# Hybrid decoder trunk on one core: the low part of every third weight tile of the mixers built by ScalarE and an accumulating DMA

## The chip, the cores and the metric

The kernel runs on one core of a Trainium2 chip. The metric is the device time of one execution in microseconds, from runs of the same program; lower is better. All profile rows come from one profiled execution.

## The reference

Two layers of a decoder trunk on 256 tokens of width 2048, all in float32. Each layer projects the normalised input once, feeds three token mixers (latent attention, a diagonal state-space layer with a GLU, dilated windowed attention), projects their normalised outputs back, and ends with a gated feed-forward block.

```python
def rms_norm(x, g):
    xf = x.astype(jnp.float32)
    y = xf * lax.rsqrt(jnp.mean(xf * xf, axis=-1, keepdims=True) + NORM_EPS)
    return (y * g.astype(jnp.float32)).astype(x.dtype)
...
for l in range(DEPTH):
    h = rms_norm(x, g_mix[l])
    proj = h @ w_in[l]
    c_q, c_kv, k_rope, u, qd, kd, vd = jnp.split(proj, split_at, axis=-1)
    y_mla = mla_mixer(c_q, c_kv, k_rope, g_q[l], w_uq[l], g_kv[l], w_ukv[l])
    y_ssm = s5_mixer(u, a_re[l], a_im[l], b_re[l], b_im[l], c_re[l], c_im[l],
                     d_skip[l], log_dt[l], w_glu[l], b_glu[l])
    y_dil = dilated_mixer(qd, kd, vd)
    y = jnp.concatenate([rms_norm(y_mla, g_out_mla[l]),
                         rms_norm(y_ssm, g_out_ssm[l]),
                         rms_norm(y_dil, g_out_dil[l])], axis=-1)
    x = x + y @ w_o[l]
    h = rms_norm(x, g_ffn[l])
    x = x + (jax.nn.silu(h @ w_gate[l]) * (h @ w_up[l])) @ w_down[l]
return rms_norm(x, g_final)
```

The three mixers are left out here: latent attention has 8 heads and low-rank projections `w_uq` and `w_ukv`; the state-space layer has 32 groups of 16 channels, a scan over the tokens, a GELU and the GLU weights `w_glu`; the dilated attention has 8 heads and three strides.

## The kernel before, in words

**Weights in two parts.** TensorE multiplies in a reduced float32 format (`float32r`). To keep float32 accuracy each operand is split into a high part, which is the operand rounded to that format, and a low part, which is the rest. `product` (L1347) makes three matmuls for each: high x high, high activation x low weight, low activation x high weight.

**Tiles and stripes.** Every weight matrix is cut into tiles of 256 rows by up to 512 columns, 720 in all. A `Stripe` is a run of tiles that accumulates one block of output columns for both halves of the tokens. `layer` (L1140) lists the stripes of a layer: first the mixers' in the order of `ORDER` (L1137), then the feed-forward's. A layer has 96 mixer tiles and 264 feed-forward tiles; tiles 0 to 95 and 360 to 455 belong to mixers. In layer 0 the stripes of `w_uq` and `w_ukv` are tiles 24 to 35, those of `w_o` for the attention 60 to 75 and for the dilated heads 76 to 83, the two GLU stripes (`g1 g0`) 84 to 87, and `w_o` for the state-space output 88 to 95.

**The pipeline of a tile.** `dma` (L1238) loads a raw tile on SP's queue into one of three buffers `wr` (`RAW`, L205). `wsplit` (L1248) takes one of four buffers each for `wh` and `wl` (`SPL`) and calls `split` (L333): ScalarE copies the raw tile to `wh`, VectorE subtracts `wh` from the raw tile and writes `wl`.

```python
            nc.scalar.activation(hi, src, AF.Copy)
            nc.vector.tensor_tensor(lo, src, hi.bitcast(F32), OP.subtract)
```

In `run` (L1260) the split of tile i + 3 is written in the middle of tile i's matmuls, and the load of the next raw tile right behind it. So a raw buffer is free again when the split of the tile in it is done, and a `wh`/`wl` buffer when TensorE is done with the tile four before.

**Side work and its planner.** The mixers themselves (transposes, attention heads, the state-space steps of `ssm`, L717, the norms) are generators that `spawn` puts on a list. Between the matmuls of weight tiles `run_side` (L285) takes the next step of a generator when its inputs are ready by the clock of a planner, `Pace` (L87), and when VectorE and ScalarE aren't too far behind TensorE by that clock (`busy`, L277). `order` (L259) sorts by how much time is left until a stripe needs the result. When a stripe needs something that isn't there, `drain` (L316) writes all the steps that are still missing ahead of the stripe's matmul. `Pace.op` (L148) books every instruction on the planner's clock; a changed booking changes the order in which side work is written on all engines. Nothing else orders it: each engine runs its instructions as written.

**Other queues.** POOL runs the Newton steps of the reciprocal roots (`rstd`, L352, twelve small instructions each), a few memsets, and eight loads. All operations are recorded at one line, L194 (a wrapper around each engine), so groups of the profile are told apart by the names of their tiles: `wr`, `wh`, `wl` for weights, `acc` for the accumulators, `pt` and `y` for the PSUM tiles of side work (`y` is the output of the state-space steps), `s` for work tiles, `one` for constants and small statistics.

## Time and profile before

| what | value |
|---|---|
| median of 3 runs | 2236.85 us (2236.36 to 2238.12) |
| the profiled execution | 2235.52 us |
| its span in the profile | 2233.5 us |
| TensorE matmul (PE) busy | 2184.5 us (98%) |
| weight load (PEld) busy | 1777.3 us (80%) |
| VectorE (DVE) busy | 1338.6 us (60%) |
| ScalarE (ACT) busy | 1046.1 us (47%) |
| GpSimd (POOL) busy | 100.5 us (5%) |
| mean granted TensorE clock | 0.992 |
| moved by DMA | 387.33 MB, 173 GB/s on average |

The profiled execution lies 1.3 us under the median. The busy times are sums over the span: an engine that is idle while another sets the pace costs nothing. The mixers of layer 0 end near 390 us; those of layer 1 lie between about 1140 and 1490 us; the rest is feed-forward.

### The profile page before, as it was taken

What the parts mean: (1) busy time and instruction counts of PE and PEld (TensorE: products, weight loads), DVE (VectorE), ACT (ScalarE), POOL (GpSimd) and SP (SyncE); (2) the same over time, 40 slices, a digit from 0 to 9 for tenths busy, and PEclk for the clock granted to TensorE, in tenths of its full rate; (3) what the DMA queues carried; (4) which work ended last, traced back from release to release, by engine and by line L of the source; (5) the groups of instructions that cost most, each with busy time, mean ns of one, the idle gap of its engine ahead of it and who ended that gap; (6) DMA issues with size and microseconds to landing.
All of it is one profiled execution on the core that took longest, in us unless ns stands there. A gap on an engine that the chain in (4) does not pass through costs nothing.

```text
span 2233.5 us, 27208 instructions
## 1 busy us (share of the span) xinstructions
PE 2184.5 (98%) x10127; PEld 1777.3 (80%) x10127; DVE 1338.6 (60%) x1967; ACT 1046.1 (47%) x1535; POOL 100.5 (5%) x283
## 2 busy tenths in 40 slices
PE   8899998999999999999999999999999999999998
PEld 6677876888788888888877778878888888888886
DVE  6976777658555445444568776674455545454555
ACT  6556433544534443344454555554444444434443
POOL 6100100000000000000001000010000000000000
PEclk9999999999999999999999999999999999999999
DMA  6443433656656655566554343456655666556654
GB/s 214 143 128 104 169 123 124 189 187 206 201 196 189 189 190 192 193 189 192 184 169 120 118 124 122 142 179 197 189 189 190 212 192 189 188 194 192 189 188 151
DMA packets 201012, 387.33 MB, mean 173 GB/s; under 512 B 12064, under 2 KB 20512, under 8 KB 200880
## 3 DMA queue, kind: packets, MB, share of 16 engines
q1 hardware_dynamic: 199696, 381.34, 53.6%
q0 software_dynamic: 1184, 4.26, 0.6%
q8 instruction: 79, 1.29, 0.2%
q14 instruction: 53, 0.43, 0.1%
HBM read 383.46 MB, written 2.10 MB: 173 GB/s over the span
## 4 chain that ended last, share of the span: by engine, by line
PE 87%; DVE 5%; ACT 2%; DMA 2%; POOL 2%; issue 2%; SPq 0%; DVEq 0%; ACTq 0%; POOLq 0%
PE acc L194 79%; PE pt L194 6%; PE y L194 3%; DVE s L194 3%; DVE wl L194 2%; POOL s L194 1%; ACT s L194 1%; ACT wh L194 1%; DMA s<-in_bT_dram 0%; POOL tn L194 0%; DMA wr<-in_w_up_dram 0%; DVE one L194 0%; DMA one<-in_params_dram 0%; DMA wr<-in_w_uq_dram 0%; DVE tn L194 0%
## 5 line engine op out<-in xcount | busy, mean ns | idle before, releaser
L194 PE MATMUL acc<-wh,s 128*128 128x512 f32 (+2 forms) x5760 | 1818.7, 391 | 12.4 <-ACT s L194 7.5
L194 DVE TENSOR_TENSOR wl<-wr,wh 128x1024 fp32r<-128x1024 f32 (+1 forms) x720 | 867.9, 1209 | 707.0 <-ACT wh L194 705.1
L194 PEld LDWEIGHTS acc<-wh,s 128*128 128x128 f32 x5760 | 1082.5, 189 | 238.7 <-issue 12.2
L194 PE MATMUL acc<-wl,s 128*128 128x512 f32 (+2 forms) x2880 | 1117.9, 388 | 9.7 <-DVE wl L194 9.7
L194 ACT ACTIVATE wh<-wr 128x1024 fp32r<-128x1024 f32 (+1 forms) x720 | 750.0, 1046 | 741.6 <-PE acc L194 692.5
L194 PEld LDWEIGHTS acc<-wl,s 128*128 128x128 f32 x2880 | 543.5, 189 | 116.8 <-DVE wl L194 14.3
L194 ACT ACTIVATE s<-pt 128x512 fp32r<-128x512 f32 (+6 forms) x138 | 68.6, 504 | 146.5 <-PE pt L194 145.9
L194 PE MATMUL pt<-one,s 128*128 128x128 f32 (+1 forms) x668 | 102.6, 273 | 12.2 <-DVE s L194 8.3
L194 PEld LDWEIGHTS pt<-one,s 128*128 128x128 f32 (+1 forms) x668 | 82.4, 140 | 36.4 <-issue 10.0
L194 DVE TENSOR_TENSOR s<-pt,s 128x512 f32<-128x512 f32 (+1 forms) x108 | 71.4, 685 | 56.3 <-ACT s L194 51.0
L194 ACT ACTIVATE s<-s 128x512 f32<-128x512 f32 (+4 forms) x162 | 80.0, 501 | 48.4 <-DVE s L194 32.1
L194 DVE TENSOR_TENSOR s<-s,s 128x512 f32<-128x512 f32 (+3 forms) x152 | 83.4, 587 | 8.9 <-ACT s L194 8.2
L194 ACT ACTIVATE s<-pt,tn 128x128 f32<-128x128 f32 (+2 forms) x128 | 44.4, 375 | 94.1 <-DVE tn L194 86.0
L194 ACT ACTIVATE s<-acc,one 128x512 f32<-128x512 f32 (+3 forms) x112 | 63.0, 604 | 36.0 <-PE acc L194 25.0
L194 PE MATMUL y<-s,one 128*32 128x256 f32 (+1 forms) x320 | 77.4, 389 | 1.0 <-DVE s L194 1.0
L194 ACT ACTIVATE s<-pt,one 128x256 fp32r<-128x256 f32 x108 | 45.9, 471 | 65.7 <-PE pt L194 65.7
L194 DVE SCALAR_TENSOR_TENSOR s<-pt,one,s 128x256 fp32r<-128x256 f32 x108 | 47.7, 478 | 40.7 <-ACT s L194 40.5
L194 DVE SCALAR_TENSOR_TENSOR s<-acc,one,s 128x512 f32<-128x512 f32 x92 | 64.5, 743 | 11.5 <-POOL one L194 11.5
L194 POOL TENSOR_TENSOR tn<-one 128x2 f32<-128x2 f32 x39 | 15.8, 406 | 1210.2 <-DVE one L194 1208.2
L194 PEld LDWEIGHTS y<-s,one 128*32 128x32 f32 (+1 forms) x320 | 33.1, 112 | 36.9 <-issue 6.9
L194 PE MATMUL pt<-s,s 128*128 128x128 f32 (+2 forms) x288 | 53.6, 309 | 2.3 <-ACT s L194 2.2
L194 PEld LDWEIGHTS pt<-s,s 128*128 128x128 f32 (+1 forms) x288 | 43.1, 193 | 7.6 <-ACT s L194 3.0
(74 smaller groups left out, 442.3 us busy)
## 6 DMA issues: line engine op xcount, KB each, us to landing
wr<-in_w_gate_dram SPq DMA_DIRECT2D x176, 512.0 KB, 3.6
wr<-in_w_up_dram SPq DMA_DIRECT2D x176, 512.0 KB, 3.5
wr<-in_w_down_dram SPq DMA_DIRECT2D x176, 512.0 KB, 4.3
wr<-in_w_in_dram SPq DMA_DIRECT2D x80, 512.0 KB, 3.6
wr<-in_w_o_dram SPq DMA_DIRECT2D x64, 512.0 KB, 3.7
wr<-in_w_uq_dram SPq DMA_DIRECT2D x16, 384.0 KB, 3.3
wr<-in_w_in_dram SPq DMA_DIRECT2D x16, 320.0 KB, 3.1
wr<-in_w_ukv_dram SPq DMA_DIRECT2D x8, 512.0 KB, 3.9
```

The source lines that it names most:

```text
L194: return f(out, *a, **k)
```

## The change

For a chosen tile, ScalarE writes the negative of the raw tile, rounded to float32r, into the low buffer; POOL issues a DMA that reads the raw tile and adds it to the low buffer in SBUF; ScalarE then copies the raw tile to the high buffer as before. VectorE's subtraction of that tile is gone. Chosen are the mixer tiles from 24 on whose number is divisible by three: 24 in layer 0, 32 in layer 1. The planner gets a booking of its own for such a DMA.

```diff
--- before.py
+++ after.py
@@ -147,7 +147,17 @@
 
     def op(self, e, op, out, ins, extra):
         st = self.t[e]
-        if op == "dma_start":
+        if op == "dma_start" and ins and ins[0].tensor.name in self.wrote:
+            for a in ins + [out]:
+                for l, h, w, we in self.wrote.get(a.tensor.name, ()):
+                    st = max(st, w + self.LAG)
+            self.t[e] = st + 900
+            n = 8
+            for s in out.shape:
+                n *= s
+            self.t["dma"] = max(self.t["dma"], st + 1000) + n / 400.0
+            end = self.t["dma"] + 1500
+        elif op == "dma_start":
             st = max(st, self.avail.get(out.tensor.name, 0.0))
             self.t[e] = st + 600
             n = 4
@@ -203,6 +213,7 @@
 
 class Trunk:
     RAW, SPL = 3, 4
+    BY_DMA = (24, 3)
 
     def __init__(self, tc, I, out, ctx, layers=DEPTH, dbg=None):
         self.pace = Pace()
@@ -1177,6 +1188,7 @@
                         out.append(Stripe(wo[1536:2048], 4, 512 * c, 512,
                                           lambda k, b: self.act4([self.dh], [self.dl])(k, b),
                                           self.o_done(l, c, "rd", then), f"dil{l}", col=c))
+        mixer = len(out)
         s0 = 0
         for gi, n in enumerate((4, 4, 3)):
             for s in range(s0, s0 + n):
@@ -1197,8 +1209,8 @@
                 out.append(Stripe(I["w_down"][l][s0 * 512:(s0 + n) * 512], 4 * n, 512 * c, 512, act,
                                   self.o_done(l, c, None, then if gi == 2 else None), f"hid{l}", 4 * s0))
             s0 += n
-        for st in out:
-            st.l = l
+        for i, st in enumerate(out):
+            st.l, st.mixer = l, i < mixer
         return out
 
     def start(self):
@@ -1254,7 +1266,12 @@
         l = self.sb.tile([128, 2, F], F32R, name=self.nm("wl"), tag="wl", bufs=self.SPL, padded_shape=[128, 2, 512])
         self.pace.alloc("wh", self.SPL, h)
         self.pace.alloc("wl", self.SPL, l)
-        self.split(h, l, r)
+        if i in self.by_dma:
+            self.nc.scalar.activation(l, r, AF.Copy, scale=-1.0)
+            self.nc.gpsimd.dma_start(l.bitcast(F32), r, accum_op=OP.add)
+            self.nc.scalar.activation(h, r, AF.Copy)
+        else:
+            self.split(h, l, r)
         self.hl_w[i] = (h, l)
 
     def run(self):
@@ -1270,6 +1287,12 @@
             self.left[f"ssm{l}"], self.left[f"dil{l}"], self.left[f"mla{l}"] = NP, 4, 4
         self.tiles = [(st.w, k, st.c0, st.F) for st in prog for k in range(0, st.kc, 2)]
         PS = self.SPL - 1
+        self.by_dma, i = set(), 0
+        for st in prog:
+            for k in range(0, st.kc, 2):
+                if i >= self.BY_DMA[0] and st.mixer and i % self.BY_DMA[1] == 0:
+                    self.by_dma.add(i)
+                i += 1
         self.setup()
         self.z = self.s4([640], BF)
         nc.vector.memset(self.z, 0.0)
```

The change moves instructions, because the planner books the chosen tiles differently. On TensorE, at the end of layer 0's mixers before the change (`wh_3389` is tile 85, the second tile of the stripe `g1`; `y` rows are state-space output):

```order
L194 MATMUL acc_3424<-wh_3389,s_1466 128x512
L194 MATMUL acc_3424<-wl_3390,s_1466 128x512
L194 MATMUL acc_3424<-wh_3389,s_1467 128x512
L194 MATMUL y_2963<-s_3303,one_85 32x256
L194 MATMUL y_2963<-s_3304,one_85 32x256 x2
L194 MATMUL y_2963<-s_3303,one_85 32x256
L194 MATMUL y_2963<-s_3183,one_86 32x256
L194 MATMUL y_2963<-s_3434,one_85 32x256
L194 MATMUL y_2963<-s_3435,one_85 32x256 x2
L194 MATMUL y_2963<-s_3434,one_85 32x256
L194 MATMUL y_2963<-s_3351,one_86 32x256
L194 MATMUL acc_3423<-wh_3389,s_1466 128x512
```

The last two of the sixteen state-space steps stand back to back inside the stripe that needs them. In the changed kernel the last `y` rows of layer 0 stand here (`wh_3068` is tile 70, `wh_3092` tile 71, both in the last `w_o` stripe of the latent attention):

```order
L204 MATMUL acc_3085<-wh_3068,s_1433 128x512
L204 MATMUL acc_3085<-wl_3069,s_1433 128x512
L204 MATMUL acc_3085<-wh_3068,s_1434 128x512
L204 MATMUL y_2515<-s_3038,one_85 32x256
L204 MATMUL y_2515<-s_3039,one_85 32x256 x2
L204 MATMUL y_2515<-s_3038,one_85 32x256
L204 MATMUL y_2515<-s_2947,one_86 32x256
L204 MATMUL acc_3084<-wh_3092,s_1433 128x512
```

The step has moved from tile 85 to tile 71. Behind it the listing has only matmuls of weight tiles until four transposes ahead of tile 88.

On SP's queue, the raw loads of tiles 84 to 90 before the change; DVE is the wait for the subtraction that frees the buffer, DMAHW a wait for an earlier load:

```order
L194 DMA wr_3286<-in_w_glu_dram 128x2x512 [waits DMAHW5_49,DVE_49]
L194 DMA wr_3312<-in_w_glu_dram 128x2x512 [waits DMAHW6_49,DVE_49]
L194 DMA wr_3334<-in_w_glu_dram 128x2x512 [waits DMAHW7_49,DVE_49]
L194 DMA wr_3371<-in_w_glu_dram 128x2x512 [waits DMAHW0_49,DVE_49]
L194 DMA wr_3393<-in_w_o_dram 128x2x512 [waits DMAHW1_49,DVE_49]
L194 DMA wr_3413<-in_w_o_dram 128x2x512 [waits DMAHW2_49,DVE_49]
L194 DMA wr_3443<-in_w_o_dram 128x2x512 [waits DMAHW3_49,DVE_49]
```

The same loads in the changed kernel; DMASW is a wait for a DMA that POOL issued, Activation one for ScalarE:

```order
L204 DMA wr_3373<-in_w_glu_dram 128x2x512 [waits DMAHW6_49,DVE_49]
L204 DMA wr_3391<-in_w_glu_dram 128x2x512 [waits DMAHW5_49,DMASW0_49]
L204 DMA wr_3413<-in_w_glu_dram 128x2x512 [waits DMAHW7_49,DVE_49]
L204 DMA wr_3432<-in_w_glu_dram 128x2x512 [waits DMAHW0_49,DMASW1_49,Activation_49]
L204 DMA wr_3454<-in_w_o_dram 128x2x512 [waits DMAHW1_49,DVE_49]
L204 DMA wr_3472<-in_w_o_dram 128x2x512 [waits DMAHW2_49,DVE_49]
L204 DMA wr_3495<-in_w_o_dram 128x2x512 [waits DMAHW3_49,DMASW2_49,Activation_49]
```

One load in three now waits for the accumulating DMA of a chosen tile. Tiles 87 and 90, chosen themselves, take the buffer of the chosen tile before them (84, 87); tile 84 takes one that VectorE has freed, and tile 85 behind it waits for the DMA of tile 81. In the listing the first pattern holds for 44 chosen tiles, the second for 12.

## Rows read from the trace of the kernel before

**Rows 1.** The page, busy time of each engine in the span.
```profile
PE 2184.5 (98%) x10127; PEld 1777.3 (80%) x10127; DVE 1338.6 (60%) x1967; ACT 1046.1 (47%) x1535; POOL 100.5 (5%) x283
```

**Rows 2.** By stage: length, PE, PEld, DVE, ACT, POOL busy; PEclk, DMA share, GB/s.
```profile
120.00:180.00 60.00, 59.83 (x323) 48.12 (x322) 40.26 (x94) 38.03 (x93) 3.12 (x6) 1.00 0.40 120
300.00:360.00 60.00, 54.15 (x239) 39.97 (x238) 48.31 (x94) 19.14 (x32) 2.91 (x13) 0.94 0.39 137
```

**Rows 3.** Timeline of PE, 318 to 375 us: start, us, instruction [idle before <-releaser].
```profile
323.12 0.69 PE L194 MATMUL pt<-one,s 128*128 128x128 f32 x2 [2.03 <-ACT s L194]
...
355.18 2.52 PE L194 MATMUL y<-s,one 128*32 128x256 f32 x10 [0.96 <-DVE s L194]
360.38 0.79 PE L194 MATMUL acc<-wh,s 128*128 128x512 f32 x1 [2.67 <-ACT s L194]
...
370.13 0.30 PE L194 MATMUL pt<-one,s 128*128 128x128 f32 x1 [1.16 <-DVE s L194]
371.37 0.55 PE L194 MATMUL pt<-one,s 128*128 128x128 f32 x3 [0.94 <-DVE s L194]
```

**Rows 4.** By stage as rows 2, finer, around those waits.
```profile
320.00:325.00 5.00, 2.41 (x12) 1.65 (x11) 3.13 (x11) 2.25 (x8) 0.00 (x0) 0.76 0.31 105
325.00:330.00 5.00, 5.00 (x14) 3.93 (x13) 3.01 (x7) 1.31 (x2) 1.02 (x6) 0.56 0.28 105
360.00:370.00 10.00, 8.59 (x30) 6.63 (x30) 6.71 (x9) 4.54 (x6) 0.00 (x0) 0.83 0.31 107
```

**Rows 5.** Groups of the page: xcount | busy us, mean ns | idle before <-releaser.
```profile
L194 DVE TENSOR_TENSOR wl<-wr,wh 128x1024 fp32r<-128x1024 f32 (+1 forms) x720 | 867.9, 1209 | 707.0 <-ACT wh L194 705.1
L194 ACT ACTIVATE wh<-wr 128x1024 fp32r<-128x1024 f32 (+1 forms) x720 | 750.0, 1046 | 741.6 <-PE acc L194 692.5
```

**Rows 6.** Timeline of PE near 101 us.
```profile
101.44 0.45 PE L194 MATMUL pt<-one,s 128*128 128x128 f32 x1 [5.29 <-DVE s L194]
```

**Rows 7.** DMA issues: queue, xcount, KB each, median us from issue to landing.
```profile
wr<-in_w_in_dram SPq DMA_DIRECT2D x80, 512.0 KB, 3.6
...
s<-in_x_dram POOLq DMA_DIRECT2D x4, 512.0 KB, 7.5
s<-in_b_glu_dram POOLq DMA_DIRECT2D x2, 512.0 KB, 4.1
```

**Rows 8.** DMA queues of the page: packets, MB, share of 16 engines.
```profile
q1 hardware_dynamic: 199696, 381.34, 53.6%
```

**Rows 9.** Timeline of SP in the feed-forward: start, us from first to last, xcount.
```profile
601.81 52.05 SPq L194 DMA_DIRECT2D wr<-in_w_down_dram  x20
```

**Rows 10.** A group of the page, transposes.
```profile
L194 PE MATMUL pt<-one,s 128*128 128x128 f32 (+1 forms) x668 | 102.6, 273 | 12.2 <-DVE s L194 8.3
```

**Rows 11.** Timeline of SP in layer 1's mixers, single issues, every third load.
```profile
1139.09 0.37 SPq L194 DMA_DIRECT2D wr<-in_w_in_dram  x1
1148.23 0.37 SPq L194 DMA_DIRECT2D wr<-in_w_in_dram  x1
1156.39 0.37 SPq L194 DMA_DIRECT2D wr<-in_w_in_dram  x1
...
1452.05 0.37 SPq L194 DMA_DIRECT2D wr<-in_w_o_dram  x1
1463.05 0.37 SPq L194 DMA_DIRECT2D wr<-in_w_o_dram  x1
1469.91 0.37 SPq L194 DMA_DIRECT2D wr<-in_w_o_dram  x1
1477.97 0.37 SPq L194 DMA_DIRECT2D wr<-in_w_gate_dram  x1
```

**Rows 12.** Timeline of POOL at 61 and 328 us, and the stage around the first.
```profile
61.12 1.22 POOL L194 TENSOR_TENSOR tn<-one 128x2 f32<-128x2 f32 x1 [15.05 <-DVE one L194]
...
328.56 0.18 POOL L194 TENSOR_TENSOR tn<-one 128x2 f32<-128x2 f32 x1 [84.02 <-DVE one L194]
...
60.00:65.00 5.00, 5.00 (x24) 4.14 (x23) 4.80 (x13) 2.17 (x3) 3.48 (x6) 1.00 0.32 74
```

## Prediction, made before the changed kernel ran

> **What bounds the kernel now.** I read the busy line first: TensorE is busy 2184.5 of 2233.5 us [rows 1]. Whatever the change does to VectorE, it can win only where TensorE waits. The table by stage says where: from 120 to 180 us TensorE works 59.83 of 60 us although VectorE is busy only 40.26, while from 300 to 360 us it works 54.15 at a granted clock of 0.94 [rows 2]. So I went on to TensorE's own waits at the end of the first mixer [rows 3]. They are waits for the state-space chain and the attention heads: 2.03 us at 323 us, 0.96 us at 355 us (on `y`, for VectorE) and 2.67 us at 360 us; 1.16 and 0.94 us at 370 us belong to the transposes of the state-space result. After such waits the granted clock falls: 0.76 and 0.56 in the ten microseconds from 320, 0.83 from 360 to 370 [rows 4], so part of that time ran at 1.2 instead of 2.4 GHz.
>
> **What the order does.** In the changed listing the planner, which now sees a freer VectorE, puts the last state-space step (four `y` rows) ahead of tile 71. Before, the last two stood together inside tile 85, in the stripe that needs them. From tile 71 on nothing but weight tiles is left for TensorE until the transposes at tile 88. The waits of 2.03, 0.96 and 2.67 us should go: 5.7 us. The clock behind them gives back at most 5 x (0.24 + 0.44) + 10 x 0.17 = 5.1 us. Gain: **10.8 us**. The work itself only moves, into stages where VectorE has 20 of 60 us free [rows 2]; I charge nothing for that. If that cover is not there, a wait on VectorE returns near 200 us.
>
> **The parts.** 56 tiles are touched: 24 of layer 0 (24 to 93), 32 of layer 1 (360 to 453).
> - VectorE loses 56 subtractions of 1209 ns, 68 us [rows 5]. Only near the start does this stand before TensorE, which waited 5.29 us for VectorE at 101 us [rows 6]. Two tiles of 768 columns (24 and 27, 0.9 us each) leave that queue: 1.8 us. Against it, tile 24's low part now comes by DMA, in a stretch with little lead. I charge about 1.2 us for that (a DMA of 384 KB for a subtraction, part of it hidden). Gain: **0.6 us**.
> - ScalarE gains 56 copies of 1046 ns, 59 us [rows 5]. It is busy 38 us of 60 from 120 us and 19 from 300 us [rows 2], so its time is covered; what is queued behind the copy comes about 1 us later.
> - POOL gains 56 DMA issues. Each waits in POOL's queue for ScalarE; the root chains of the norms stand behind it, and it behind them. The listing leaves most without such a neighbour; 0.
> - SP: a load into the raw buffer of a chosen tile now waits until the accumulating DMA has landed, and the loads behind it in SP's queue wait too. This is the term that decides.
>
> **The turn of a raw buffer.** Load 3.6 us [rows 7], negative copy 1.06 us (1046 ns, [rows 5]), the accumulating DMA, about 0.2 us for hand-overs (an estimate). The trace has no accumulating DMA. Nearest below: a plain copy of 512 KB issued by POOL lands in 4.1 us; nearest above: such copies in a burst of four, 7.5 us [rows 7]. An addition must read its target too. A second pass over 512 KB is worth 1.5 us: 53.6% of 16 engines over 2233.5 us for 199696 packets is 96 ns a packet of 2 KB, and an engine has 16 of them [rows 8]. I take 4.1 + 1.5 = **5.6 us**, nearer to the single copy because only one is under way at a time. The turn is 3.6 + 1.06 + 5.6 + 0.2 = **10.5 us**. By the Trainium skill (DMA: Bandwidth & Descriptors, the anatomy of a DMA from GpSimd) a copy costs about 2.0 us plus bytes over 436 GB/s, 3.2 us here, against the 4.1 us of the trace; with the bytes read twice its estimate is 4.4 us, and the sum below would end near 2225.
>
> TensorE's own pace in pure weight tiles is 19 steps in 52.05 - 0.37 us, 2.72 us a tile or **8.2 us** for three [rows 9]. Where side work lies between the tiles the turn hides: in layer 1 the mean spacing of three loads is 338.9 us / 30 = 11.3 us [rows 11]. In pure stretches it doesn't, if a chosen tile is loaded into the buffer of the chosen tile before. The listing of SP shows that this is so for 44 of the 56. For 12, most of them in the pure stretches (72, 78, 81, 84; 438, 441, 444, 450, 453), the chosen tile gets the buffer that a subtraction has freed, and the load after it waits for the DMA. Such a turn isn't closed and I charge nothing. A split may start three tiles ahead of its use, so a stretch begins with 8.2 - (1.06 + 5.6 + 0.2) = 1.3 us in hand.
> - Layer 0, the closed turns from 84 to 93: 3 x (10.5 - 8.2) = 6.9 us, less 1.3 in hand, less the 2.1 us for the state-space transposes [rows 3], which stay, and ten transposes of 0.154 us (102.6 us / 668, [rows 10]): **2.0 us**.
> - Layer 1, start: SP's issues, which follow TensorE, stand 9.14 and 8.16 us apart [rows 11]; 21.0 - 17.3 - 1.3 = **2.4 us**.
> - Layer 1, end: of the spacings 11.00, 6.86 and 8.06 [rows 11] one short turn (444 to 447) is closed; 10.5 - 6.86 - 1.3 = **2.3 us**.
>
> Sum: 2.0 + 2.4 + 2.3 - 10.8 - 0.6 = -4.7 us on the profiled 2235.52 us, 2230.8. The median of the runs shown is 1.3 us above that execution, so **2232 us**, 0.2% faster. (About 0.2%, 4.5 us, is what a measurement of this kernel can tell from no change.) So large an edit comes to little because it frees VectorE mostly where TensorE did not wait for it.
>
> **Bounds.** With 4.1 us the turn is 9.0 us, 2.8 in hand, and costs nothing; tile 24 is then hardly late: 2237 - 10.8 - 1.8 = 2224. With 7.5 us the turn is 12.4 us, above even the mean spacing of layer 1: 25 closed turns x 1.1 = 28 and some 20 more because long spacings can't lend all their surplus to short ones, 9 + 10 in layer 0, so 2237 + 67 - 11 = 2293.
>
> **Rivals.**
> - *The addition is quicker* (chance 0.22): at 4.6 us the turn is 9.5, 2.3 in hand; layer 1 pays about 0.2, 2237 - 11.2 = **2226 us**. For it: both ends are in SBUF, while the 4.1 us copy read DRAM. The Trainium skill's estimate, above, lies on this side.
> - *As summed* (0.24): 5.1 to 5.6 us, 2228 to 2232, the likeliest case's own range.
> - *Neither* (0.18): 5.6 to 6.3 us, 2233 to 2241.
> - *The addition collides with the raw loads* (0.26). The three loads of a turn and the addition share 16 engines that are already busy half the time [rows 8]. It decides from a landing of about 6.1 us on (turn 11.0, 0.8 in hand: 4.0 + 3.9 + 3.3 = 11.2 against 11.4). At 6.5 us, turn 11.4, 0.4 in hand: layer 0 pays 9.6 - 0.4 - 3.6 = 5.6, the start 5.1, the end 4.5, and closed turns at the mean spacing some 8: 2237 + 23 - 11 = **2249 us**, slower.
> - *The gain of the order isn't there* (0.05): VectorE can't keep up with the earlier chain and the drain stays late; 2232 + 10.8, **2243**.
> - *POOL is held up by VectorE* (0.05). Steps of the root chains on POOL took 0.18 us at 328 us and 1.22 us at 61 us, where VectorE was busy 4.80 of 5 us [rows 12]. One delay of 1.2 us per issue makes the turn 11.7 us: 6.8 + 6.0 + 5.4 and about 8 at the mean spacing, 2237 + 26 - 11 = **2252**. The Trainium skill (SBUF — State Buffer, who interferes with whom) says that POOL and VectorE share a port pair which one of them can hold for a whole instruction; the stretched steps agree, no DMA issue in the trace shows it.
>
> That makes 0.46 faster, 0.18 same, 0.36 slower. The range of 8 in 10 runs from the plain copy's price to an addition near 7 us: 2223 to 2264.
>
> **What would show it.** Right: accumulating DMAs landing in 5 to 5.8 us; no `y` of layer 0 after about 305 us and the clock near 1.00 from 320 to 370; waits of 1 to 3 us for `wl` only between tiles 84 and 93 and at both ends of layer 1; VectorE about 68 us less, ScalarE 59 more, feed-forward stages unchanged. Wrong: landings over 6 us, or waits for `wl` in the middle of the mixers (tiles 36 to 60, 387 to 432), where side work should cover them.

## The result, and the profile after

The changed kernel takes **2269.43 us** (median of 4 runs, 2266.82 to 2270.53); the kernel before takes 2236.61 us beside it (2235.04 to 2238.12). The ratio is 1.0148, 95% interval 1.0135 to 1.016: 33 us slower. The forecast was 2232 us, with a range up to 2264. The time lies above the range and on the other side of no change.

The page of the changed kernel: busy time of each engine, the DMA queues, two groups with low parts, and three kinds of transfer (KB each, median us from issue to landing).

```profile
PE 2194.7 (97%) x10127; PEld 1781.9 (79%) x10127; DVE 1280.0 (56%) x1911; ACT 1100.5 (49%) x1591; POOL 147.7 (7%) x339
...
q1 hardware_dynamic: 199696, 381.34, 56.1%
q0 software_dynamic: 10272, 32.44, 7.4%
...
L204 PE MATMUL acc<-wl,s 128*128 128x512 f32 (+2 forms) x2880 | 1121.3, 389 | 34.5 <-DMA wl<-wr 26.5
...
L204 POOL DMA_DIRECT2D wl<-wr x56 | 51.3, 916 | 1246.8 <-ACT wl L204 1114.6
...
wr<-in_w_in_dram SPq DMA_DIRECT2D x80, 512.0 KB, 4.4
wr<-in_w_o_dram SPq DMA_DIRECT2D x64, 512.0 KB, 4.5
wl<-wr POOLq DMA_DIRECT2D x48, 512.0 KB, 4.9
```

VectorE lost 58.6 us (forecast 68) and ScalarE gained 54.4 us (forecast 59) [rows 1]. The addition lands in 4.9 us, sooner than the 5.6 us that I took. A raw load of `w_in` takes longer: 4.4 us where it took 3.6 us [rows 7]. Not all of that is the additions': without them, in the same order (e9 below), it takes 3.8 us, and the loads of `w_gate`, which have no addition beside them, took 3.6 us before, 4.3 in the changed kernel, 3.9 in e9 and 4.4 in e11. TensorE waits 26.5 us for low parts that come by the DMA. The span grew from 2233.5 to 2267.6 us. Of these 34.1 us TensorE idles 23.9 us more (72.9 against 49.0), and its busy time is 10.2 us longer, at a mean granted clock of 0.987 (before 0.992).

TensorE's waits of the changed kernel (us in total, times, longest us):

```profile
PE acc L204 <- DMA wl<-wr: 26.5, 15, 5.3
PE pt L204 <- ACT s L204: 12.0, 7, 4.9
PE pt L204 <- DVE s L204: 10.7, 7, 4.1
PE acc L204 <- DVE wl L204: 7.9, 9, 2.5
```

The waits of [rows 3] at 323, 355 and 360 us are gone, as forecast. In their place stand waits for the DMA and two for side work. They are in TensorE's timeline:

```profile
91.92 0.69 PE L204 MATMUL acc<-wl,s 128*128 128x384 f32 x1 [5.28 <-DMA wl<-wr]
...
239.72 0.50 PE L204 MATMUL acc<-wl,s 128*128 128x512 f32 x1 [1.35 <-DMA wl<-wr]
275.55 0.48 PE L204 MATMUL pt<-one 128*128 128x384 bf16 x1 [4.89 <-ACT s L204]
...
378.26 0.50 PE L204 MATMUL acc<-wl,s 128*128 128x512 f32 x1 [2.30 <-DMA wl<-wr]
385.20 0.44 PE L204 MATMUL pt<-one,s 128*128 128x128 f32 x1 [4.14 <-DVE s L204]
...
1457.31 0.50 PE L204 MATMUL acc<-wl,s 128*128 128x512 f32 x1 [2.77 <-DMA wl<-wr]
...
1497.25 0.79 PE L204 MATMUL acc<-wl,s 128*128 128x512 f32 x1 [2.87 <-DMA wl<-wr]
```

The stages as in [rows 2], with DMA share and GB/s at the end:

```profile
300.00:360.00 60.00, 57.89 (x264) 43.97 (x263) 35.69 (x66) 25.93 (x37) 8.13 (x19) 1.00 0.79 215
360.00:420.00 60.00, 50.61 (x219) 39.87 (x218) 32.42 (x50) 31.75 (x50) 7.52 (x18) 0.91 0.68 186
1440.00:1500.00 60.00, 51.58 (x221) 40.73 (x220) 28.40 (x41) 29.30 (x37) 12.62 (x33) 0.97 0.79 218
```

The second of these stages before the change:

```profile
360.00:420.00 60.00, 56.22 (x247) 44.95 (x248) 40.21 (x61) 33.93 (x61) 7.51 (x25) 0.94 0.45 143
```

From 300 to 360 us the clock is back at 1.00 and TensorE busier than before (54.15): the forecast gain is there, and the next stage gives it back (50.61 against 56.22). The DMA share has doubled, from 0.39 to 0.79.

### The profile page after: what moved, and what is told of

The parts are those of the page before. It is cut to its first block, busy times and chain, and to the rows that moved or that the text cites. A ratio compares the mean times of both kernels' runs of the same rounds, so it can differ in the third digit from the quotient of the medians.

```text
span 2267.6 us, 27346 instructions
## 1 busy us (share of the span) xinstructions
PE 2194.7 (97%) x10127; PEld 1781.9 (79%) x10127; DVE 1280.0 (56%) x1911; ACT 1100.5 (49%) x1591; POOL 147.7 (7%) x339
## 3 DMA queue, kind: packets, MB, share of 16 engines
q1 hardware_dynamic: 199696, 381.34, 56.1%
## 4 chain that ended last, share of the span: by engine, by line
PE 81%; DMA 7%; DVE 5%; ACT 3%; POOL 2%; issue 2%; SPq 0%; ACTq 0%; DVEq 0%; POOLq 0%
PE acc L204 73%; PE pt L204 6%; DMA wl<-wr 3%; PE y L204 3%; DVE s L204 3%; DVE wl L204 2%; POOL s L204 1%; ACT s L204 1%; DMA wr<-in_w_in_dram 1%; ACT wh L204 1%; ACT wl L204 1%; DMA s<-in_b_glu_dram 1%; DMA wr<-in_w_o_dram 1%; DMA wr<-in_w_glu_dram 0%; DMA s<-in_bT_dram 0%
## 5 line engine op out<-in xcount | busy, mean ns | idle before, releaser
L204 DVE TENSOR_TENSOR wl<-wr,wh 128x1024 fp32r<-128x1024 f32 (+2 forms) x664 | 803.4, 1212 | 732.7 <-ACT wh L204 724.7
L204 PE MATMUL acc<-wl,s 128*128 128x512 f32 (+2 forms) x2880 | 1121.3, 389 | 34.5 <-DMA wl<-wr 26.5
L204 POOL DMA_DIRECT2D wl<-wr x56 | 51.3, 916 | 1246.8 <-ACT wl L204 1114.6
L204 ACT ACTIVATE wl<-wr 128x1024 fp32r<-128x1024 f32 (+2 forms) x56 | 57.2, 1022 | 58.2 <-DMA wr<-in_w_o_dram 18.3
```

The source lines that it names most:

```text
L204: return f(out, *a, **k)
```

## Experiments

Differences are of medians, each against the kernel before on the same chip; one text on record has 10.3 us for the plain copy, which it took from the ratio (the medians differ by 10.9), and 34.1 us for the change, the difference of the profiled spans (32.8 by the medians). The names of the theories: T1 is the turn of a raw buffer (it is free later, so the loads come later), T2 the order, T3 the order's need of a freer VectorE, T4 contention (transfers slow each other), T5 the low part's own latency, T6 ScalarE's copies, T7 the DMA engines' own time (they have no room for the additions).

| run | us | against before | ratio, 95% interval |
|---|---|---|---|
| e1, order alone | 2237.56 | +2.2 | 1.0001 to 1.0019 |
| e2, transfers in the old order | 2258.43 | +23.1 | 1.0087 to 1.0114 |
| e3, fourth raw buffer | 2244.89 | +9.6 | 1.0025 to 1.005 |
| e3b, the same for before | 2244.50 | +9.2 | 1.0028 to 1.0053 |
| e4, plain copy | 2245.91 | +10.9 | 1.0033 to 1.0059 |
| e5, old order, from tile 36 | 2255.93 | +20.9 | 1.0077 to 1.0104 |
| e6, traffic only | 2257.50 | +22.5 | 1.0079 to 1.011 |
| e7, hold only | 2261.43 | +26.4 | 1.0103 to 1.013 |
| e8, ScalarE's copy only | 2243.18 | +6.8 | 1.0022 to 1.0049 |
| e9, no DMA | 2227.56 | -8.8 | 0.9952 to 0.9977 |
| e3c, fourth buffer, same order | 2254.26 | +17.9 | 1.0072 to 1.0099 |
| e11, the same for before | 2235.23 | -1.1 | 0.9986 to 1.0003 |
| e12, covered tiles, old order | 2241.82 | +6.6 | 1.0021 to 1.0046 |
| e13, uncovered tiles, old order | 2247.21 | +12.0 | 1.0037 to 1.0062 |
| e14, covered tiles, planned | 2242.64 | +7.4 | 1.0023 to 1.0048 |
| e15, every sixth tile | 2247.58 | +12.3 | 1.0043 to 1.007 |
| e16, layer 0 only | 2227.25 | -7.8 | 0.9951 to 0.9978 |
| e17, layer 0 only, late fourth load | 2223.33 | -11.7 | 0.9936 to 0.9961 |

### The order and the transfers apart: e1, e2

`self.pace.op` books an operation with the planner, `self.tc.nc` issues one without booking. So the order of one kernel can be kept while the work of the other is done.

```diff
 e1, against the changed kernel:
-            self.nc.scalar.activation(l, r, AF.Copy, scale=-1.0)
-            self.nc.gpsimd.dma_start(l.bitcast(F32), r, accum_op=OP.add)
-            self.nc.scalar.activation(h, r, AF.Copy)
+            nc = self.tc.nc
+            self.pace.op("scalar", "activation", l, [r], [])
+            self.pace.op("gpsimd", "dma_start", l.bitcast(F32), [r], [])
+            self.pace.op("scalar", "activation", h, [r], [])
+            nc.scalar.activation(h, r, AF.Copy)
+            nc.vector.tensor_tensor(l, r, h.bitcast(F32), OP.subtract)
 e2, against the changed kernel:
+            nc = self.tc.nc
+            self.pace.op("scalar", "activation", h, [r], [])
+            self.pace.op("vector", "tensor_tensor", l, [r, h.bitcast(F32)], [])
-            self.nc.scalar.activation(l, r, AF.Copy, scale=-1.0)
+            nc.scalar.activation(l, r, AF.Copy, scale=-1.0)
-            self.nc.gpsimd.dma_start(l.bitcast(F32), r, accum_op=OP.add)
+            nc.gpsimd.dma_start(l.bitcast(F32), r, accum_op=OP.add)
-            self.nc.scalar.activation(h, r, AF.Copy)
+            nc.scalar.activation(h, r, AF.Copy)
```

> The instructions stand in the changed kernel's order on every engine, but VectorE subtracts for the chosen tiles as before: no negative copy and no accumulating DMA. T1 (the loss of 33 us is TensorE's wait for low parts that come by a DMA, and the longer turn of a raw buffer): the transfers are gone, so the waits of TensorE for wl by a DMA (26.5 us) are gone and the raw loads are back at a median of 3.6 us (w_in); the time is -10 to +8 us of the kernel before, by how much of the -10.8 us of the new order stands against VectorE's extra work. T2 (the new order itself costs: its waits at 275 and 385 us of the changed kernel are set by the order): both waits are there, of 4 to 5 us each, and the time is +10 to +20 us. T3 (the new order needs the relief of VectorE): neither wait as it was, but waits of TensorE on VectorE for wl or s near 200 to 320 us, 5 to 15 us more in all, and the time is +5 to +15 us.

> The low parts of the chosen tiles come from the negative copy and the accumulating DMA as in the changed kernel, but all instructions of TensorE stand in the order of the kernel before. T1 (transfer and turn): the waits of TensorE for wl by a DMA are as many as in the changed kernel, 20 to 32 us, raw loads of w_in at 4.4 us, and the time is +25 to +40 us of the kernel before. T2 (the order): the waits at 275 and 385 us of the changed kernel are gone (near 370 us again at most 1.2 us), and the time is +5 to +20 us. T3: as T1, and more by the old order's own waits at 323, 355 and 360 us (5.6 us), +30 to +42 us.

**Measured.** e1 +2.2 us, e2 +23.1 us. TensorE's order in e1 is the changed kernel's row for row, in e2 that of the kernel before. The order alone brings nothing; the transfers, with ScalarE's copies and VectorE's relief, cost most of the loss. The two sum to 25 us and the change costs 33, so they also make each other worse, by 7.5 us that no run takes apart. In e1 the late waits of [rows 3] are gone: its stage from 300 to 360 us has TensorE busy throughout. But other waits came, here in its stages and its timeline:

```profile
300.00:360.00 60.00, 60.00 (x272) 47.80 (x271) 42.30 (x61) 24.87 (x35) 3.68 (x14) 1.00 0.60 193
```

```profile
88.81 0.33 PE L204 MATMUL pt<-one,s 128*128 128x128 f32 x1 [2.48 <-ACT s L204]
...
1229.22 0.45 PE L204 MATMUL pt<-one,s 128*96 128x128 f32 x2 [5.26 <-ACT s L204]
```

e1 lies in T1's range and under those of T2 and T3. e2 lies in none: 1.9 us under T1's, with 18.9 us of waits for low parts where T1 had 20 or more, 3.1 over T2's and 6.9 under T3's. So T2 falls as the main cause and T1 fits best. T3 missed both ranges; its idea comes back with e9.

### How long the transfer is: e4, e9

```diff
 e4:
-            self.nc.gpsimd.dma_start(l.bitcast(F32), r, accum_op=OP.add)
+            self.nc.gpsimd.dma_start(l.bitcast(F32), r)
 e9:
-            self.nc.gpsimd.dma_start(l.bitcast(F32), r, accum_op=OP.add)
+            self.pace.op("gpsimd", "dma_start", l.bitcast(F32), [r], [])
```

> The changed kernel, in its order, with a plain copy of the raw tile by the same DMA in place of the accumulating one; the addition is left out, so the low part is the raw tile. It prices the accumulation. If the addition makes the transfer long: landings of 512 KB fall from 4.9 to about 4.1 us (the single copy of the kernel before that stands nearest), a turn of a raw buffer from 10.7 to 9.9 us, TensorE's waits for wl by a DMA from 26.5 to 14 to 20 us, and the time to +18 to +27 us of the kernel before. If the price is that of any transfer between SBUF and SBUF beside the loads: landings 4.6 to 5.0 us, waits 22 to 30 us, time +28 to +37 us.

> The changed kernel, in its order, without the accumulating DMA: the low part is the negative copy alone; the addition is left out. It is the end of the row of transfers 4.9 us (+34.1 us), 3.0 us (+10.3 us), 0 us. T1 and T5 (the transfer's time decides): no wait for wl by a DMA, raw loads bind nothing, VectorE is relieved of 56 subtractions: -8 to +2 us of the kernel before. T6 (ScalarE's copies cost by themselves): +8 to +15 us, about where the plain copy is, with its waits for s of 24 us.

**Measured.** Both leave the addition out; the order is the changed kernel's in both. Landing of 4.9 us: +32.8 us. Of 3.0 us: +10.9. No transfer: -8.8. So 41.6 us hang on the additions' DMAs alone. The step from a plain copy to an addition makes more than half of them: 1.9 us of landing, the longer time on the DMA engines (below) and 0.34 us more of POOL for each issue, which these runs don't part. Both theories for the plain copy had its landing too long (4.1 us or more) and its time too high. The plain copy's queue, group, landing and wait:

```profile
q0 software_dynamic: 8928, 32.44, 3.8%
...
wl<-wr POOLq DMA_DIRECT2D x48, 512.0 KB, 3.0
...
PE acc L204 <- DMA wl<-wr: 9.6, 9, 2.9
```

The page gives what a transfer costs the 16 engines. Without such transfers q0 has 0.6% (the page before, where all of q0 is 4.26 MB). An addition is (7.4 - 0.6)% of 2267.6 us over 56, **2.75 us of all 16 engines** (a mean; eight of the 56 are smaller than 512 KB). A plain copy is (3.8 - 0.6)% of 2243.8 us over 56, 1.28 us. A raw load of 512 KB is 56.1% of 2267.6 us x 0.524 MB / 381.34 MB, 1.75 us. Three loads and an addition make 8.0 us, and TensorE needs three pure tiles every 8.2 us [rows 9]. With a plain copy it is 6.5 us. Whether the engines are full by this sum (T7) is taken up with the next runs.

### A fourth raw buffer: e3, e3b, e3c, e11

```diff
 e3, e3b:
-        r = self.sb.tile([128, 2, F], F32, name=self.nm("wr"), tag="wr", bufs=self.RAW,
+        r = self.sb.tile([128, 2, F], F32, name=self.nm("wr"), tag="wr", bufs=self.RAW + 1,
...
-            if s < 2:
+            if s < 3:
                 load()
 e3c, e11; dma issues without booking, plan books the load as before:
-            self.dma(nd)
+            self.dma(nd + (ns >= 12))
+            if ns == 11:
+                self.dma(nd + 1)
+            self.plan(nd)
```

> The changed kernel with a fourth raw buffer and one raw load more ahead; the order on TensorE is not touched. T1 (the loss is the turn of a raw buffer, 10 to 11 us against TensorE's 8.2 us for three tiles): with four buffers a turn may take four tiles, 10.9 us, so the waits of TensorE for wl by a DMA fall from 26.5 us to under 12 us (those that stay come from single late landings), and the time falls from +33 us to +5 to +18 us of the kernel before. T4 (the loss is contention: the loads and the additions slow each other in SBUF, whatever waits for them): more loads in flight make the landings longer, the waits stay at 20 us or more, and the time stays at +25 to +40 us. T2 (order): the waits at 275 and 385 us stay with 4 to 5 us each in either case.

> The control of the run before this: the kernel before with a fourth raw buffer and one raw load more ahead. T1: raw loads bound nothing in the kernel before, so within 5 us of it (-5 to +5). T4 (contention): a load more in flight makes the loads longer, but nothing waits for them: 0 to +5 us. If it is faster by over 5 us, the kernel before waited for raw loads and the fourth buffer's gain in the changed kernel is not the turn's alone.

> The changed kernel with a fourth raw buffer from tile 12 on, and its order on TensorE kept word for word (in the earlier run with four the planner saw the early load and 2118 of 9240 of TensorE's rows stood elsewhere). T1 (the turn of three buffers decides): ScalarE's negative copies no longer wait for raw loads, TensorE's waits for wl by a DMA fall from 26.5 us to 12 to 18 us, and the time to +8 to +18 us of the kernel before. T4 (contention): the landings grow from 4.9 to 6 us or more, the waits stay over 20 us and the time at +20 us or more.

> The control: the kernel before with a fourth raw buffer from tile 12 on, its order on TensorE kept. If the +9.2 us of the earlier control came from the load at the start and from the order: -3 to +3 us. If a raw load more in flight costs by itself (it lands beside the loads of constants and slows them): +5 to +12 us.

**Measured.** In e3 and e3b the order was not untouched, as the texts claim: the planner saw the early load, and some 2100 and 1400 of TensorE's rows stand elsewhere. Their +9.6 and +9.2 us tell little. In e3c and e11 the order is kept row for row. The control is -1.1 us, within the noise, so the kernel before lost nothing to its raw buffers. The changed kernel falls from +32.8 to +17.9. The third buffer's turn (T1) is thus worth 15 us in this order. But 17.9 us stay, and TensorE's waits for the DMA, which by T1 should have fallen to 12 to 18 us, are as long as with three buffers:

```profile
PE acc L204 <- DMA wl<-wr: 26.2, 14, 5.9
...
PE pt L204 <- ACT s L204: 5.1, 3, 4.1
```

What fell is the wait for ScalarE's side work, from 12.0 to 5.1 us, and the lower clock (TensorE busy 2187.6 instead of 2194.7 us). The additions from 328 to 362 us, four in each, of the changed kernel and then of e3c:

```profile
DMA to landing us min/median/max: 5.0/5.6/7.2
```

```profile
DMA to landing us min/median/max: 8.3/8.5/9.0
```

and the stage from 330 to 370 us, in the same order:

```profile
330.00:370.00 40.00, 37.05 (x161) 29.67 (x160) 19.81 (x23) 17.87 (x18) 4.00 (x5) 1.00 0.80 221
```

```profile
330.00:370.00 40.00, 34.01 (x146) 26.76 (x145) 15.31 (x17) 15.16 (x15) 3.99 (x5) 1.00 0.81 217
```

With a fourth buffer the loads wait less for the addition. Here they run beside it, the addition lands 3 us later, and the DMA share stays at 0.8. That is so in places only: the median landing of all 48 additions of 512 KB went from 4.9 to 5.1 us, not to the 6 us of T4. And 0.8 is not the most that the engines give. From 1460 to 1470 us the changed kernel has:

```profile
1460.00:1470.00 10.00, 10.00 (x45) 8.08 (x44) 4.64 (x6) 4.84 (x6) 1.42 (x2) 1.00 1.03 305
```

The share adds up the times of packets, and a share above 1 says that these overlap. So transfers do slow each other (T4), but that the engines have no room for the additions (T7, the 8.0 of 8.2 us) is not shown.

### What the change puts on the other engines: e6, e7, e8

```diff
 e8, in the old order; q is a spare buffer:
+            nc.scalar.activation(q, r, AF.Copy, scale=-1.0)
             nc.scalar.activation(h, r, AF.Copy)
             nc.vector.tensor_tensor(l, r, h.bitcast(F32), OP.subtract)
 e6, behind the copy to q:
+            nc.gpsimd.dma_start(q.bitcast(F32), self.cst[:, None, :F].to_broadcast([128, 2, F]), accum_op=OP.add)
 e7, behind the copy to q:
+            for _ in range(2):
+                nc.gpsimd.dma_start(q[:, 0, :8].bitcast(F32), r[:, 0, :8])
```

> The kernel before with the changed kernel's extra load and nothing that waits for it: for each chosen tile ScalarE's negative copy goes to a spare buffer, and a DMA adds 512 KB of a constant to that buffer; the raw buffer is not read by the DMA and the low part is VectorE's subtraction as before. The order on TensorE is the one before. Compare with +23.1 us of the old order with the DMA for the low parts. T1 (turn of the raw buffer) and T5 (the low part's own latency, from the cut to the landing): -2 to +6 us. T4 (contention: DMA bytes and ScalarE's copy slow raw loads and VectorE): raw loads of w_in at 4.4 us as there, TensorE waits for DVE wl and s 10 us longer, and +10 to +23 us.

> The kernel before with the raw buffer held longer and almost no traffic: for each chosen tile ScalarE's negative copy goes to a spare buffer, then two DMAs of 32 bytes a partition read the raw buffer one after the other (the second waits for the first), about 4 to 5 us in all; the low part is VectorE's subtraction as before, in the old order. T1 (turn): the loads behind the held buffer come late, TensorE waits for DVE wl or ACT wh 8 to 20 us more, time +8 to +20 us. T4 (contention) and T5 (latency of the low part): 0 to +5 us. If both this and the run with traffic only stay under +5 us, T5 is what is left.

> What the runs with traffic only (+22.5 us) and with the held buffer (+26.4 us) have in common: the kernel before, in its order, with ScalarE's negative copy of each chosen tile to a spare buffer, and no DMA. T6 (ScalarE: 56 copies of 1.06 us, in front of the high part and of whatever stands behind it on ScalarE, make the state-space and attention steps late): +10 to +24 us, with the waits of TensorE for s near 1472 and 1507 us that both runs showed. T1 and T4 (it was the hold there and the bytes here): -2 to +6 us, and those waits are not there.

**Measured.** ScalarE's copies alone cost 6.8 us, between the two ranges. Traffic alone makes it 22.5 us, the hold alone 26.4 us, though no low part waits for a DMA in either. So by these runs each of T4 and T1 costs 15 to 20 us beside the copies, and they can't be added: the transfer that does both, and relieves VectorE, costs 23.1 us in this order. Three limits. There is a single spare buffer, for which ScalarE once waited 10.1 us in e6, just ahead of a wait of TensorE of 5.33 us. e6's transfers are heavier than the change's: they land in 5.9 us and take (8.9 - 0.6)% of 2259.4 us over 56, 3.35 us of all 16 engines. And both runs put issues into POOL's queue, ahead of loads that stand in it: the GLU bias of layer 0 is issued at 355.83 us in e6 and at 360.52 in e7, against 331.80 before. Neither run is the bytes or the hold alone. All three runs show a wait of 3.7 to 5.9 us for a late `s` of VectorE near the end of layer 1, where before has none over 2.0 us; here with the copies alone:

```profile
1461.96 0.76 PE L204 MATMUL acc<-wh,s 128*128 128x512 f32 x1 [3.69 <-DVE s L204]
```

### Where it costs: e5, e12, e13, e14, e15

```diff
 e5, old order:
-    BY_DMA = (24, 3)
+    BY_DMA = (36, 3)
 e12 (old order) and e14 (planned):
-                if i >= self.BY_DMA[0] and st.mixer and i % self.BY_DMA[1] == 0:
+                if i >= self.BY_DMA[0] and st.mixer and i % self.BY_DMA[1] == 0 and (36 <= i < 84 or 384 <= i < 435):
 e13, old order, in the same place:
+                if i >= self.BY_DMA[0] and st.mixer and i % self.BY_DMA[1] == 0 and (84 <= i < 384 or 435 <= i):
 e15:
-    BY_DMA = (24, 3)
+    BY_DMA = (24, 6)
```

> As the run in the old order with the DMA for the low parts (+23.1 us), but the first chosen tile is 36: tiles 24, 27, 30 and 33 get theirs from VectorE as before. In that run tile 24 waited 4.60 us for its DMA, and its lead over the kernel before, tile by tile, stood at +5.1 us from there to tile 42. If that loss is not made up later: +16 to +20 us, and no wait for wl by a DMA before tile 36. If it lies beside something that comes late anyway (the wait of 5.2 us for VectorE's s just after it stays): +20 to +24 us. If VectorE, not relieved there, makes the state-space steps late: over +24 us.

> As the run in the old order with the DMA for the low parts (+23.1 us), but only for the 33 chosen tiles that have state-space or attention work of TensorE beside them (36 to 81, 384 to 432); the rest get theirs from VectorE. T7 (a low part by DMA keeps the 16 DMA engines busy for about 2.75 us, a raw load for 1.77 us: three tiles and an addition 8.1 us, all of TensorE's 8.2 us where nothing is beside the weights): covered turns cost nothing, -2 to +5 us. T6 (ScalarE's 33 copies, by the +6.8 us of 56 copies): +4 us and more, up to +10 us.

> The complement of the run before this: the old order, and only the 19 chosen tiles with little beside them (84 to 93, 360 to 381, 435 to 453) get their low part by the DMA. T7: the cost is here, +11 to +18 us, turns of a raw buffer of 10 us and more and a DMA share near 0.8. T6: a third of the copies, +2 to +5 us beside the waits for wl by a DMA.

> The changed kernel with only the 33 covered tiles chosen, and the order left to the planner (1659 of 9240 of TensorE's rows stand elsewhere than in the changed kernel, 1761 elsewhere than before). It is the candidate for a gain. T7: the covered turns are free and VectorE is relieved where the state-space steps run: -6 to +2 us. T6, or covered turns that are late all the same: +3 to +12 us.

> The changed kernel with every sixth tile in place of every third (28 additions), the order left to the planner. T7: six tiles and one addition keep the DMA engines for 6 x 1.77 + 2.75 = 13.4 us of TensorE's 16.4 us, so no turn is bound by them; waits for wl by a DMA 5 to 9 us, of which 4 to 5 are tile 24's; time -2 to +8 us. If each addition costs alike wherever it stands (latency, ScalarE), half of the changed kernel's loss: +14 to +19 us.

**Measured.** The 19 tiles with little beside them cost 12.0 us (0.63 each, in T7's range), the 33 covered ones 6.6 us (0.20 each, in T6's), the four early ones 2.2 us (e2 less e5, within the noise of the two). A copy on ScalarE alone costs 6.8 / 56 = 0.12 us each, so T6 has a part and isn't enough. That a tile costs most where little stands beside it fits T1 and T7 alike; these runs don't part them. e14 doesn't gain: TensorE's transposes wait 14.5 us for ScalarE's `s` in it, against 4.2 us before. e15 falls between its two theories. It has only five waits for the DMA, 14.2 us in all: tile 24 (4.26 us), at 145 us (2.04), at 1397 us (0.62), at 1465 us (3.25), and this one:

```profile
339.42 0.79 PE L204 MATMUL acc<-wl,s 128*128 128x512 f32 x1 [4.04 <-DMA wl<-wr]
```

Its addition was ready at 323.0 us but stood in POOL's queue behind twelve small instructions of a root chain that came at 329.49 us, and was issued at 334.81:

```profile
329.49 0.55 POOL L204 TENSOR_TENSOR tn<-one 128x2 f32<-128x2 f32 x1 [24.12 <-DVE one L204]
...
334.81 0.90 POOL L204 DMA_DIRECT2D wl<-wr  x1 [0.34 <-issue]
```

So a single addition that is late for a reason of its own costs TensorE 4 us with half as many of them, too. That the DMA engines have more room then is argued.

### A version that is faster: e16, e17

```diff
 e16, against e3:
-                if i >= self.BY_DMA[0] and st.mixer and i % self.BY_DMA[1] == 0:
+                if i >= self.BY_DMA[0] and st.mixer and st.l == 0 and i % self.BY_DMA[1] == 0:
 e17, against e16; dma books the load, fetch issues it:
             self.dma(nd)
+            if nd == 15:
+                self.fetch(14)
+            if nd != 3:
+                self.fetch(nd - (3 < nd < 15))
```

> The first run with a fourth raw buffer (+9.6 us; its planner saw the early load, so its order differs) with the additions in layer 0 only; layer 0 is word for word as there, layer 1 is the planner's. In that run's profile TensorE led the kernel before by 5.4 us when layer 0's last tile was through, after a loss of 4.0 us up to tile 18, and lost 10.7 us in layer 1. T7 (the transfers of layer 1 cost those 10.7 us): -8 to 0 us. If layer 1 loses by the order that follows from layer 0 and not by its transfers: +3 to +10 us.

> As the run before this, in the same order, but the fourth raw buffer is loaded from tile 12 on and not among the loads of x at the start. If the 4.0 us up to tile 18 are the early load's: 2 to 5 us less than the run before this, -12 to -3 us of the kernel before. If the loss at the start is the order's (a step of TensorE moved there): the same within 1.5 us.

**Measured.** -7.8 and -11.7 us: both faster than either kernel. Leaving the additions out of layer 1 is worth 17.4 us against e3 (the order of layer 1 moves with them: some 1100 of TensorE's rows stand elsewhere), and issuing the fourth load later 3.9 us, in the same order. What part of e17's gain is the additions', the fourth buffer's or the order's is open: no run has that order with VectorE's subtractions. TensorE waits 6.8 us for low parts by the DMA in it.

## Why the prediction was wrong

It can be read as two terms. Without the transfers it had -10.8 - 1.8 = -12.6 us; e9 measured **-8.8**. For the transfers it had 1.2 + 2.0 + 2.4 + 2.3 = 7.9 us; from e9 to the changed kernel they measured **41.6**. The second is the step that failed. Between the two profiled executions lie 40.1 us: TensorE idles 30.1 us more in the changed kernel, and 26.5 us of its idle time are waits for low parts by the DMA; its busy time is 10.0 us longer (2194.7 against 2184.7), at a mean granted clock of 0.987 against 0.993. Where it failed can be read tile by tile, because both have the same order: TensorE's first product with each tile's low part, in the changed kernel less the same in e9 (profiled executions, us).

```
tiles       forecast   measured
  0 to  24    +1.2       +5.0
 24 to  60     0         +1.1
 60 to  66     0         +6.4
 66 to  84     0         +4.5
 84 to  92    +2.0       +6.3
 92 to 359     0         -0.6
359 to 372    +2.4       +5.1
372 to 430     0         -0.7
430 to 456    +2.3      +13.0
456 to 719     0          0.0
sum           +7.9      +40.1
```

**The turn of a raw buffer: its length was right, by two errors.** ScalarE's negative copies stand 10.4 us apart at the start of layer 1 (1143.17 to 1174.47 us, three turns), against 10.5 forecast. The addition was quicker (4.9 instead of 5.6 us), and the loads slower (4.4 instead of 3.6). The landing came out between the rival of the quicker addition (4.6 us, 2226 us) and the case as summed (5.1 to 5.6, 2228 to 2232); the time was some 40 us above both. So the price of one landing was not what decided. ScalarE's timeline of the changed kernel shows the turn; the wait is for the raw load:

```profile
1143.17 1.06 ACT L204 ACTIVATE wl<-wr 128x1024 fp32r<-128x1024 f32 x1 [0.72 <-PE acc L204]
1153.77 1.06 ACT L204 ACTIVATE wl<-wr 128x1024 fp32r<-128x1024 f32 x1 [3.87 <-DMA wr<-in_w_in_dram]
1163.72 1.06 ACT L204 ACTIVATE wl<-wr 128x1024 fp32r<-128x1024 f32 x1 [2.65 <-DMA wr<-in_w_in_dram]
1174.47 1.06 ACT L204 ACTIVATE wl<-wr 128x1024 fp32r<-128x1024 f32 x1 [5.61 <-DMA wr<-in_w_in_dram]
```

**"Such a turn isn't closed and I charge nothing": this failed, and so did the time in hand of the closed ones.** TensorE's 26.5 us are 5.28 at tile 24, 4.5 at tiles with an open turn (81: 0.83, 84: 1.27, 441: 0.96, 444: 1.48), where nothing was charged, and 16.7 at tiles with a closed turn, where 6.7 were. An open turn delays the load behind the chosen tile's buffer, and SP's queue delays all behind that one. So tile 444 itself came late, and the closed turn behind it had no 1.3 us in hand: at tile 447 TensorE waited 2.87 us instead of 2.3, and its granted clock stood at 0.66 from 1495 to 1505 us, so that the loss from tile 446 to 449 is 6.1 us. Tile 435, a closed turn that nothing was charged for, cost 2.77. At the start of layer 1 I had counted two turns; a third of the same length made it 5.1 us. Three raw loads and an addition take 8.0 of 8.2 us of the DMA engines. The loads' part of that was in [rows 8]; I used it to price the addition, and didn't ask whether it fits. That this sum is what makes the low parts late is not shown.

**"Where side work lies between the tiles the turn hides": mostly right.** 24 to 60 cost 1.1 us and 372 to 430 nothing, although tile 381 waits 2.84 us: e9 waits 2.27 us there for side work. 60 to 66 cost 6.4 us, and that shows how a late load reaches TensorE without any low part being late. ScalarE's timeline, of the changed kernel and then of e9, at the same place of the order:

```profile
267.55 1.06 ACT L204 ACTIVATE wh<-wr 128x1024 fp32r<-128x1024 f32 x1 [5.66 <-DMA wr<-in_w_o_dram]
268.51 1.25 ACT L204 ACTIVATE sv<-acc,one 128x512 f32<-128x512 f32 x2
```

```profile
257.66 1.06 ACT L204 ACTIVATE wh<-wr 128x1024 fp32r<-128x1024 f32 x1 [1.91 <-DMA wr<-in_w_o_dram]
258.62 1.25 ACT L204 ACTIVATE sv<-acc,one 128x512 f32<-128x512 f32 x2
```

The time from issue to landing of the raw load that ScalarE waits for, in the same order:

```profile
DMA to landing us min/median/max: 7.8/7.8/7.8
```

```profile
DMA to landing us min/median/max: 4.1/4.1/4.1
```

It was issued at 259.67 us, while an addition was under way (issued at 257.52 us, landed at 262.52), so it did not wait for that addition's landing: it was slow beside it and beside a load of x that POOL had issued at 258.11 and that landed at 266.69. ScalarE stood 5.66 us at the high part of a tile that was not chosen; the attention step behind it came late, and TensorE's 4.89 us at 275.55 follow. In e9 ScalarE waits 1.91 us for the load, and TensorE 1.15. With a fourth buffer (e3c) the load is as slow, 7.18 us, but this stretch costs nothing against e9.

**POOL, "the listing leaves most without such a neighbour; 0": this failed.** POOL has nine loads, not eight as I had written, and the x loads and the GLU bias stand in its queue behind additions that wait for ScalarE. The changed kernel, then e9:

```profile
257.52 0.85 POOL L204 DMA_DIRECT2D wl<-wr  x1 [12.93 <-DVE one L204]
...
258.11 1.09 POOL L204 DMA_DIRECT2D s<-in_x_dram  x1
...
372.76 0.87 POOL L204 DMA_DIRECT2D wl<-wr  x1 [10.50 <-ACT wl L204]
373.30 0.91 POOL L204 DMA_DIRECT2D s<-in_b_glu_dram  x1
```

```profile
230.18 2.31 POOL L204 DMA_DIRECT2D s<-in_x_dram  x3
...
317.87 0.57 POOL L204 DMA_DIRECT2D s<-in_b_glu_dram  x1
```

So the load of x came into the stretch of tile 60, and the bias, 55 us later than in e9, landed at 379.48 us, when VectorE had been waiting for it:

```profile
379.57 1.29 DVE L204 TENSOR_TENSOR s<-acc,s 128x512 f32<-128x512 f32 x2 [3.98 <-DMA s<-in_b_glu_dram]
```

TensorE's transposes behind that work wait 4.14 us at 385.20 and 0.79 us at 386.44, against 0.92 and 0.94 in e9. That, and 2.30 us for tile 87's low part, make the stretch from 84 to 92 cost 6.3 us instead of 2.0. In e17 VectorE waits 5.62 us for the same bias. No run issues these loads from another queue, so what POOL's queue costs in all is not measured.

**Tile 24: mis-sized.** 1.2 us were charged; its addition landed in 8.3 us, beside two raw loads and a load of the state-space constants, and TensorE waited 5.28 us. The wait of [rows 6] fell to 3.54 us, so net it was 5.0 at tile 24 and less behind.

**"ScalarE's time is covered": wrong in part.** 56 copies alone cost 6.8 us in the old order.

**The order: right in what it moves, wrong that the rest is free.** The waits went and the clock came back (e1's stage from 300 to 360 us), and yet the order alone is 2.2 us slower than before. "I charge nothing" for the moved work failed: in e1 it meets waits for ScalarE at 89 and 1229 us. It pays only when VectorE is relieved: from e1 to e9 lie 11.0 us, in the same order. The forecast had put nearly all its gain on the order and 1.8 us on the relief.

**The rivals.** The collision with the raw loads (2249 us, chance 0.26) came nearest in kind and was still 20 us low: the median landing stayed below the 6.1 us from which I let it decide, while single loads and additions took 7 to 8 us beside each other. Its sum has 4.5 us for the end of layer 1 where its terms give 4.1 (11.4 - 6.86 - 0.4), and POOL's has 5.4 where they give 4.7; neither moves a price by more than 1 us. POOL's delay (0.05) was seen, by another mechanism than the one I had: in the changed kernel one addition stood 7.77 us behind a root chain that waited for VectorE, and cost TensorE 1.35 us at 239.72, and loads stood behind additions, as above. VectorE holding a port is not shown; the order of POOL's queue was enough.

By the Trainium skill (DMA: Bandwidth & Descriptors, Queues, rings and completion order) each DMA engine takes turns between the queues that have work for it, packet by packet, so a load beside an addition gets only a part. The traces agree: the load above went from 4.1 us in e9 to 7.8 beside an addition and a load of x, and the additions from 328 to 362 us went from 5.6 to 8.5 us when a fourth buffer let them meet the loads. That page's formula (Anatomy of one DMA) gave an estimate of 3.2 us for the copy and 4.4 us for the addition; measured were 3.0 and 4.9, with 4.5 where nothing ran beside it.

The two signs that I had named for a wrong forecast came only faintly: the median landing is under 6 us, with nine of the 56 above it, and in the middle of the mixers two low parts are late, by 1.35 and 0.36 us. They watched the addition and not the loads behind it.

What stays open: how the 26.7 us that a fourth buffer doesn't give back (17.9 + 8.8) divide between contention among the transfers, the low part's own latency, ScalarE's knock-on and POOL's queue.

## What to carry to other kernels

Before work moves from an engine to a DMA, look beyond the landing of a single transfer. Add up what the DMA engines have to do in the stretch where nothing else is beside them (queue share times span over transfers, for the loads and for the new transfer) and set it against the time that the bound engine needs there; a sum that comes near it, as 8.0 of 8.2 us here, is a warning that transfers will slow each other, not yet a proof. A buffer that is released later delays every load behind it in an in-order queue, and through the engine that waits for that load also work that has nothing to do with the transfer: ask at each turn who stands behind it, not only whether it closes. Ask the same of the queue that issues the new transfer: whatever it issues later now waits for the transfer's inputs. And put such a change only where the relieved engine's work reaches the end: in layer 0 alone, with a fourth buffer, the same transfer stands in a kernel that is 11.7 us faster.

## What the runs showed of the hardware

- An accumulating DMA of 512 KB within SBUF lands in 4.9 us (median, 4.5 where it is alone) and a plain copy in 3.0 us. By the packets' times it takes 2.75 us of all 16 engines against 1.28 us (means of 56, eight of them smaller), more than twice, and more than a raw load of 512 KB (1.75 us).
- Its issue holds POOL longer as well: 916 ns in the mean against 577 ns for the plain copy.

```profile
L204 POOL DMA_DIRECT2D wl<-wr x56 | 32.3, 577 | 1237.3 <-ACT wl L204 1090.9
```

- The share of the DMA engines in the profile is no share of a whole: over 10 us it reached 1.03, at 305 GB/s.
- Additions to a spare buffer and a hold of the raw buffer with almost no bytes cost nearly the same (22.5 and 26.4 us, 6.8 of each for ScalarE's copies), with the limits given there.
- A load that POOL issues stands behind the DMAs ahead of it in POOL's queue until their inputs are there: the GLU bias was issued at 373.30 us instead of 317.87 (e9).
